# Mixers: four more output rows with seven block products instead of eight, and one ordered block for gate stage and output projection

## The chip, the cores and the metric

The kernel runs on 1 core of a Trainium2 chip. The metric is device time in microseconds (us) of one execution. The median of 3 runs of the kernel before is 2486.89 us (2486.2 to 2486.92).

The engines are named as the profile names them: PE (matmul; PEld is its weight load), DVE (elementwise on two operands), ACT (elementwise on one operand, with functions such as the sigmoid), POOL and SP (here nearly all of their work is the issue of transfers). Each works through its own queue in order and waits on semaphores for the others.

## What is computed

Two layers, each with a feed-forward half step, a mixer and a second feed-forward half step, on 640 tokens (512 of a prompt and 128 of running streams), width 1024. The change is in the mixer. Cut to what matters:

```python
z = h @ w_in                                   # conv B | conv C | conv V | q | k | v | gates
cb, cc, cv, q, k, v, g = split(z)
g_conv, g_attn = split(sigmoid(g + b_gate))    # 1024 columns each
y_conv = cb * causal_depthwise_conv3(cc * cv)  # 512 columns
y_attn = chunk_band_attention(q, k, v)         # 512 columns
m = g_conv * (y_conv @ w_conv_out) + g_attn * (y_attn @ w_attn_out)
x = x + m @ w_o
```

All of it is float32.

## The kernel before

**Layout.** Activations lie transposed: 128 features on the partitions, 640 tokens along the row. `x[m]` is the m-th of 8 such tiles (KT = 8), `y_conv` and `y_attn` have 4 (CT = 4). Weights come as a stream of 128 x 1024 "slabs", eight 128 x 128 blocks each, one transfer of 512 KB on SP's queue per slab.

**Three products for one.** Every float32 operand is split in two parts, `hi` (a rounded copy, made by ACT, "CAST whi") and `lo` (what is left, made by DVE, "wlo<-raw,whi"). A product is the sum hi·hi + hi·lo + lo·hi. A matmul instruction takes 128 x 128 weights and 320 tokens (HT, half of the row), so one weight block on all tokens is 6 instructions.

**Eight or seven block products.** A plain product (`product`, line 434) sums its weight blocks over all k. The other form treats a product as 2 x 2 blocks (even and odd feature tiles, first and second half of the tokens) and uses seven block products instead of eight, after Strassen and Winograd. It needs mixtures of the operand's quarters (names N6, T7, T4, T5) and of the weights. The weight mixtures are made by DVE on the two raw slabs of a group ("raw<-raw", "s<-raw,raw") and by POOL, which loads one slab onto another with an adding transfer ("one<-in_wst"). Such a group has 2 raw slabs and gives 4 prepared ones, where two plain slabs give 2.

**The gate stage** (`outputs`, one per layer, after the attention) is what changes. It works through, in this order:
- gate pairs: `gate_pair(m)` makes gates m and m+1 of the 16 from h. Seven block products of 12 instructions each on PE, into banks named qa, qb and qc. Gates 0 and 1 are made earlier.
- `out(m)`: one row tile of `y_conv @ w_conv_out` (m below 8) or `y_attn @ w_attn_out` (8 to 15), 24 instructions in bank py, then a multiplication by the gate and, for the attention, an addition into `mm[m - 8]`, both on DVE.
- `rows("co", (4, 5, 6, 7))`: the convolution's rows 4 to 7 at once, by seven block products: 84 instructions, banks rb, ra and rc.

The order before is: pair 2, out 0 to 3, pairs 4 and 6, `rows("co")`, then four times a pair and two outs (pair 8, out 8, out 9, and so on to out 15). `give` then splits the sums `mm` into hi and lo, as inputs of w_o. Last, the output projection: eight products `po` of 48 instructions each, each followed by an addition to x on DVE and by `ex.final(m)`, which prepares the next feed-forward's operands.

**What sets the order.** PE, DVE and ACT have their order written out by hand here (`manual_schedule`): their instructions stand in the queue as the code issues them. Callbacks put work between block products: `at[0..2]` in a gate pair, `due()` and `lates` for what is put off to the next unit. `prep` issues the next slab's casts on ACT, `flush` the pending lo parts on DVE, `ahead` and `source` the weight mixtures. The pool `tp` (tag t) has 4 temporaries for gates, `acc` has 2 double banks (py, po, ra, rb), `att` 4 banks.

**Names.** In listings raco and rbco are the banks of `rows("co")`, capsm, c and rs are staging tiles, ya and yc are `y_attn` and `y_conv` (yc tiles are used again as `mm[4..7]`), m_0hi is the hi part of m's tile 0, `thi` and `hhim` are operands of the gate pairs.

Of the kernel before, what the change touches and what calls it, by code (L numbers as in the profile page):

```python
# [11 lines left out]
F32R = mybir.dt.float32r  # L12
# [4 lines left out]
P = 128  # L17
# [178 lines left out]
def trunk(ctx: ExitStack, tc: tile.TileContext, xin, wst, small, pbias, samplebias, kcache, vcache, gfin,  # L196
# [1136 lines left out]
    def mixer(l, after):  # L1333
        with tc.tile_pool(name=f"yp{l}", bufs=1, reuse_waits="tile") as yp, \
# [83 lines left out]
            layout(f"g{l}", 1)  # L1418
            with tc.tile_pool(name=f"gp{l}", bufs=1, reuse_waits="tile") as gp, \
                 tc.manual_schedule(engines=ORDERED):  # L1420
# [3 lines left out]
        with tc.manual_schedule(engines=ORDERED):  # L1424
            hold[0] = True
            for m in range(KT):
                po = acc(f"po{l}_{m}")
                product(po, mo)
                ex.weights(m)
                DVE.tensor_tensor(out=halves(x[m]), in0=two(po), in1=halves(x[m]), op=ALU.add)  # L1430
                if m < KT - 1:
                    flush()
                ex.final(m)
        return ex
# [50 lines left out]
    def outputs(l, gp, X, st, cs, ycp, yas, sigmoid, gates):  # L1485
# [20 lines left out]
        def gate_pair(m, at):  # L1506
            n = f"{l}_{m}"
            pa, pb, pc = (att(f"q{i}{n}")[:, :HT] for i in "abc")
            u, g = gates[m], gates[m + 1] = tmp(f"g{n}"), tmp(f"g{n}_1")
            s0 = quiet()  # L1510
            block(pa, s0, 0, X11, every, True, True)
            ACT.copy(c1, pa)
            due()
            prep(used[0] + 1)
            flush()
# [51 lines left out]

        yc, ya, mo = [], [], []
        more = []
        yas_ = [yas[:, c, :] for c in range(CT)]  # L1570

# [3 lines left out]

        def give(ms):
            for m in ms:
                mo.append(parts(hp, "h", f"m{l}_{m}", mm[m]))

        def low(lo, z, hi):  # L1580
            DVE.tensor_tensor(out=lo, in0=z, in1=hi.bitcast(F32), op=ALU.subtract)

        def mixed(i, y, z):

            z = z.rearrange("p c (a b) -> p (c a) b", a=2)
            e1, e2, o1, o2 = (z[:, i] for i in range(4))
            add(e1, e1, e2, ALU.subtract)
            add(e2, o2, e2, ALU.subtract)
            for out, a in ((o2, e1), (o1, o2)):
                DVE.scalar_tensor_tensor(out=out, in0=a, scalar=-1.0, in1=out, op0=ALU.mult, op1=ALU.subtract)  # L1590
            yield
            hi, lo = (gp.tile([P, 3, HT], F32R, tag=f"x{i}{p}", name=f"x{p}{l}_{len(more)}") for p in ("hi", "lo"))
            ACT.copy(hi, z[:, 1:])
            more.append((hi, lo))
            yield
            low(lo, z[:, 1:], hi)
            yield
            hi, lo = (u[:, t2] for u in y[2 * i])
            ACT.copy(hi, e1)
            yield  # L1600
            low(lo, e1, hi)
            yield

        def take_even(c, src):
            y = tuple(gp.tile([P, T], F32R, tag=f"y{c}{i}", name=f"ya{l}_{c}{i}") for i in ("hi", "lo"))
            split(*(z[:, t1] for z in y), src[:, t1])
            ya.append(y)

        EXTRA = XT7, XT4, XN6

        def kind(y, i, k):
            if k in EXTRA:
                return tuple(z[:, EXTRA.index(k)] for z in more[i - 2])
            hi, lo = y[2 * i + (k in (X21, X22))]
            return tuple(z[:, t2 if k in (X22, XT5) else t1] for z in (hi, lo))

        def rows(name, ms, y, then=None):

# [7 lines left out]
            def mul(ps, s, half, k, start):  # L1626
                for u in range(2):
                    for i in range(2):
                        kp = half * NP + 2 * u + i
                        wh, wl = (z[:, kp * P : (kp + 1) * P] for z in s)  # L1630
                        xh, xl = kind(y, i, k)
                        for j, (w, x_) in enumerate(((wh, xh), (wh, xl), (wl, xh))):
                            PE.matmul(ps[u], w, x_, start=start and i == 0 and j == 0,
                                      stop=i == 1 and j == 2, skip_group_check=True)
# [18 lines left out]
            prep(used[0] + 1)  # L1653
            flush()
            mul(b, w, 1, X21, True)
            add(s1, two(B), s1)
# [3 lines left out]
            ACT.copy(s2, two(A))  # L1660
            gated(0, [s1[:, u] for u in range(2)], t1)
            mul(c, w, 1, XT5, True)
            for u in range(2):
# [5 lines left out]
            ahead()  # L1669
            gated(1, [s5[:, u] for u in range(2)], t2, -1.0)  # L1670
            mul(c, w, 1, X22, False)
# [3 lines left out]
            gated(0, [s2[:, u] for u in range(2)], t2)  # L1675
            if then:
                then()
            if name == "co":
                moved(0)
            mul(a, w, 0, XT4, False)  # L1680
            flush()
            gated(1, a, t1, -1.0)
            if name == "co":
                lates.append(lambda: moved(1))

        def total(m0, m1):
            for m in range(m0, m1):
                add(mm[m], mm[m], gates[KT + m])

        none = lambda: None  # L1690

        def also(*fs):
            return lambda: [f() for f in fs]

        def going(z):
            return lambda: next(z)

        gate_pair(2, [none, none, lambda: take(yc, "yc", range(CT), ycs)])
        z = [mixed(i, yc, ycp[i]) for i in range(2)]
        out(0, yc, None, going(z[0]))  # L1700
        out(1, yc, None, also(going(z[0]), going(z[1])))
        out(2, yc, None, also(going(z[0]), going(z[1])))
        out(3, yc, None, going(z[1]))
        both = also(going(z[0]), going(z[1]))
        gate_pair(4, [both, both, none])
# [665 lines left out]
```

## Time and profile before

| | us |
|---|---|
| median of 3 runs | 2486.89 |
| the profiled execution | 2487.08 |
| its span, first to last instruction | 2485.3 |
| PE busy | 2471.0 (99%) |
| DVE busy | 2158.3 (87%) |
| ACT busy | 1373.0 (55%) |
| POOL busy | 317.4 (13%) |

The profiled execution took 1.78 us more than its span and 0.19 us more than the median. Its mean granted PE clock is 0.999 of full speed. The gate stage and w_o of layer 0 lie at about 634 to 833 us of the span, those of layer 1 at about 1866 to 2064 us.

A matmul's row shows a start and a duration; matmuls overlap, so what one costs on a full PE is the distance from its start to the next start, not its duration. The same holds, to a smaller degree, for DVE and ACT. In a timeline, "[0.96 <-PE raco L1633]" after a row says how long the engine was idle before it, and what ended the wait.

### The profile page before, as it was taken

Reading aid. Unit: us, or ns where it says so; the run is one execution under the profiler, and the core shown is the slowest. Engines: PE = TensorE matmul, PEld = TensorE weight load, DVE = VectorE, ACT = ScalarE, POOL = GpSimd, SP = SyncE. Lnnn points to the kernel's source line nnn. Section 1 sums busy time; section 2 is a strip of 40 time slices with the busy share of each in tenths; the row PEclk is TensorE's granted clock in tenths of the full one; section 3 lists DMA queues with packets and bytes.
Section 4 is the critical chain, followed back from the end, with each engine's and each line's share of the span. In section 5 each row is a group of like instructions: output and inputs, shape, how many; then the busy total and the mean of one; then the engine's idle time right before and its main releaser. Section 6 shows DMA issues by size and latency. Waiting matters only on the chain.

```text
span 2485.3 us, 43991 instructions
## 1 busy us (share of the span) xinstructions
PE 2471.0 (99%) x17288; PEld 2418.2 (97%) x17288; DVE 2158.3 (87%) x3587; ACT 1373.0 (55%) x2196; POOL 317.4 (13%) x479
## 2 busy tenths in 40 slices
PE   9999999999999999999999999999999999999999
PEld 8999999889999999999999999998999999999998
DVE  7999998888886899998799999988878769999997
ACT  6555556665554555555665555556645455555555
POOL 0111112211000001111001111121110000111111
PEclk9999999999999999999999999999999999999999
DMA  4443445335343334444334443453453333443444
GB/s 155 126 118 102 123 119 121 113 109 177 104 118 108 94 101 106 112 117 120 108 94 109 110 118 102 116 128 107 132 173 92 115 111 89 107 116 106 113 117 117
DMA packets 113072, 287.11 MB, mean 116 GB/s; under 512 B 12928, under 2 KB 52480, under 8 KB 112864
## 3 DMA queue, kind: packets, MB, share of 16 engines
q1 hardware_dynamic: 69552, 220.10, 28.0%
q0 software_dynamic: 42880, 63.94, 13.7%
q8 instruction: 135, 2.21, 0.4%
q14 instruction: 73, 0.60, 0.1%
q10 hardware_dynamic: 432, 0.25, 0.0%
HBM read 238.43 MB, written 7.94 MB: 99 GB/s over the span
## 4 chain that ended last, share of the span: by engine, by line
PE 92%; DVE 4%; ACT 2%; DMA 1%; issue 1%; SPq 0%; DVEq 0%; ACTq 0%; POOLq 0%
PE pab L458 12%; PE paa L458 11%; PE pcb L458 6%; PE daa L1143 6%; PE pca L458 5%; PE dab L1143 5%; PE po L434 5%; PE qa L458 4%; PE py L434 3%; PE pbb L458 3%; PE dca L1143 3%; PE pba L458 3%; PE dcb L1143 2%; PE ma_qk L458 2%; PE ma_cv L458 2%; PE pv L1770 2%
## 5 line engine op out<-in xcount | busy, mean ns | idle before, releaser
L363 ACT CAST whi<-raw 128x512 fp32r<-128x512 f32 (+1 forms) x573 | 500.4, 878 | 371.3 <-PE pbb L458 46.0
L368 DVE TENSOR_TENSOR wlo<-raw,whi 128x512 fp32r<-128x512 f32 (+1 forms) x573 | 574.4, 1005 | 135.9 <-ACT whi L363 132.1
L363 ACT CAST whi<-s 128x1024 fp32r<-128x1024 f32 (+1 forms) x160 | 151.6, 947 | 313.3 <-issue 111.4
L458 PE MATMUL pab<-xhib,whi 128*128 128x320 f32 x704 | 217.5, 309 | 0.0
L458 PE MATMUL pab<-xlob,whi 128*128 128x320 f32 x704 | 217.0, 308 | 0.0
L458 PE MATMUL pab<-xhib,wlo 128*128 128x320 f32 x704 | 217.0, 308 | 0.0
L458 PE MATMUL paa<-xhia,whi 128*128 128x320 f32 x640 | 197.7, 309 | 0.2 <-DVE ga L295 0.2
L458 PE MATMUL paa<-xhia,wlo 128*128 128x320 f32 x640 | 197.5, 309 | 0.0
L458 PE MATMUL paa<-xloa,whi 128*128 128x320 f32 x640 | 197.4, 308 | 0.0
L368 DVE TENSOR_TENSOR wlo<-s,whi 128x1024 fp32r<-128x1024 f32 (+1 forms) x160 | 174.8, 1092 | 4.6 <-ACT whi L363 4.6
L1165 POOL DMA_DIRECT2D x<-c_a x80 | 70.0, 1022 | 573.8 <-ACT ahia L1047 205.5
L1165 POOL DMA_DIRECT2D x<-c_b x72 | 62.8, 1002 | 583.6 <-ACT ahib L1047 205.8
L458 PEld LDWEIGHTS pab<-xhib,whi 128*128 128x128 f32 x704 | 132.1, 188 | 0.9 <-issue 0.9
L458 PEld LDWEIGHTS pab<-xlob,whi 128*128 128x128 f32 x704 | 132.2, 188 | 0.0
L458 PEld LDWEIGHTS pab<-xhib,wlo 128*128 128x128 f32 x704 | 132.1, 188 | 0.0
L458 PEld LDWEIGHTS paa<-xhia,whi 128*128 128x128 f32 x640 | 120.1, 188 | 1.1 <-DVE ga L295 0.5
L458 PEld LDWEIGHTS paa<-xloa,whi 128*128 128x128 f32 x640 | 120.1, 188 | 0.2 <-DVE xloa L702 0.2
L458 PEld LDWEIGHTS paa<-xhia,wlo 128*128 128x128 f32 x640 | 120.1, 188 | 0.2
L295 DVE TENSOR_TENSOR raw<-s,raw 128x512 f32<-128x512 f32 x160 | 109.1, 682 | 0.0
L458 PE MATMUL pcb<-xhib,wlo 128*128 128x320 f32 x352 | 108.7, 309 | 0.0
L458 PE MATMUL pcb<-xlob,whi 128*128 128x320 f32 x352 | 108.5, 308 | 0.0
L458 PE MATMUL pcb<-xhib,whi 128*128 128x320 f32 x352 | 108.5, 308 | 0.0
(840 smaller groups left out, 8150.4 us busy)
## 6 DMA issues: line engine op xcount, KB each, us to landing
raw<-in_wst SPq DMA_DIRECT2D x375, 512.0 KB, 3.6
x<-c_a POOLq DMA_DIRECT2D x80, 160.0 KB, 4.6
x<-c_b POOLq DMA_DIRECT2D x72, 160.0 KB, 3.6
lent<-in_wst POOLq DMA_DIRECT2D x36, 256.0 KB, 3.9
kc<-in_kcache SPq DMA_DIRECT2D x32, 256.0 KB, 5.2
vc<-in_vcache SPq DMA_DIRECT2D x16, 512.0 KB, 4.8
one<-in_wst POOLq DMA_DIRECT2D x28, 256.0 KB, 4.1
x<-u_a POOLq DMA_DIRECT2D x40, 160.0 KB, 4.1
```

What stands on the lines that cost most here:

```text
L295: DVE.tensor_tensor(out=out, in0=a, in1=b, op=op)
L363: ACT.copy(hi[:, d], src[:, c])
L368: DVE.tensor_tensor(out=lo, in0=src, in1=hi.bitcast(F32), op=ALU.subtract)
L434: PE.matmul(ps[:, a, :HT], w, x[a] if isinstance(x, tuple) else x[:, a * HT : (a + 1) * HT], start=first and j == 0 and not seeded, stop=l ...
L458: PE.matmul(ps, a, b, start=start and kp == 0 and j == 0, stop=stop and kp == NP - 1 and j == 2, skip_group_check=True)
L1143: PE.matmul(ps[u], w, y, start=start and i == 0 and j == 0, stop=i == 1 and j == 2, skip_group_check=True)
L1165: POOL.dma_start(x[ms[2 * u + r]][:, cols], z[:, u], accum_op=ALU.add)
L1770: PE.matmul(pv[t], xx[:, t * P : (t + 1) * P], w[:, kk * AW : (kk + 1) * AW], start=c == 0 and kk == 0 and j == 0, stop=c == KT // 2 - 1 a ...
```

## The change

**Attention's rows 4 to 7 by seven.** `out(12)` to `out(15)` go. Pairs 12 and 14 follow each other, and `rows("ao", (4, 5, 6, 7))` stands after them. The mixtures of `y_attn` that it needs are made from its raw tiles in place (`mix`, four DVE instructions), and split into hi and lo (`high` on ACT, `rest` on DVE), all as callbacks of out 8 and of pairs 10, 12 and 14.

**Mixtures in tiles of their own.** Those of the convolution were one tile of three mixtures for each of two feature pairs; now each mixture has a tile that holds both pairs. For the convolution each is cast and split by itself (320 columns, six instructions on each engine, before two of 960).

**Sums and splits.** The sums of rows 4 to 7 are added after `rows("ao")` (`total`), those of m's tiles 0 to 3 are split earlier, in pair 14 and in `rows("ao")` (`given`).

**Copies.** `rows("co")` copies its four results from gate tiles to yc tiles (`moved`, on ACT). The first two copies used to stand before `qa_8`'s first copy; now they stand behind it, and the other two come in pair 8's second callback.

**w_o.** Gate stage and w_o are one ordered block. The first two products take their slabs together and run in two halves each: po_0 and po_1 with m's tiles 0, 2, 1, 3, then both with 4 to 7.

The number of raw slabs is the same; each layer has two more prepared slabs. Outside the gate stage and w_o the queues are the same, instruction by instruction.

```diff
-    for i in range(4):
+    for i in range(2):
         out += [gates[4 + i], ("ao", 2 * i), ("ao", 2 * i + 1)]
+    out += gates[6:] + [("rows", ("ao", (4, 5, 6, 7)))]
     return out + [("o", m) for m in range(KT)]
...
+        first = [acc(f"po{l}_{m}") for m in range(2)]
+        ws = [[tiles.take() for _ in mo] for _ in first]
+        for ks in ((0, 2, 1, 3), range(KT // 2, KT)):
+            for p, w in zip(first, ws):
+                for k in ks:
+                    multiply(p, w[k], mo[k], k == 0, k == KT - 1)
+        for m in range(KT):
+            po = first[m] if m < 2 else acc(f"po{l}_{m}")
+            if m > 1:
                 product(po, mo)
...
+        def room(name):
+            for k in EXTRA:
+                x[name, k] = tuple(gp.tile([P, 2, HT], F32R, tag=f"x{EXTRA.index(k)}{i}",
+                                           name=f"x{i}{name}{l}_{EXTRA.index(k)}") for i in ("hi", "lo"))
...
-            ACT.copy(hi, z[:, 1:])
-            more.append((hi, lo))
+            for k in EXTRA:
+                ACT.copy(x["co", k][0][:, i], z[:, 1 + EXTRA.index(k)])
...
+        za = yas.rearrange("p (i c) (a b) -> p i (c a) b", i=2, a=2)
+
+        def mix(n):
+
+            e1, e2, o1, o2 = (za[:, :, k] for k in range(4))
+            if n == 0:
+                add(e1, e1, e2, ALU.subtract)
+            elif n == 1:
+                add(e2, o2, e2, ALU.subtract)
+            else:
+                minus(*((o2, e1) if n == 2 else (o1, o2)))
+
+        def place(k):
+            if k == XT5:
+                return [(*(u[:, t2] for u in ya[2 * i]), za[:, i, 0]) for i in range(2)]
+            return [(*x["ao", k], za[:, :, 1 + EXTRA.index(k)])]
+
+        def high(*ks):
+            for k in ks:
+                for hi, _, z in place(k):
+                    ACT.copy(hi, z)
+
+        def rest(*ks):
+            for k in ks:
+                for hi, lo, z in place(k):
+                    low(lo, z, hi)
...
-            if name == "co":
-                moved(0)
...
             if name == "co":
-                lates.append(lambda: moved(1))
+                lates.append(lambda: moved(0))
+                moves.append(lambda: moved(1))
...
-        rows("co", (4, 5, 6, 7), yc)
-        for m in range(KT, 2 * KT, 2):
-            last = m == 2 * KT - 2
-            gate_pair(m, [none, none, (lambda: take(ya, "ya", range(CT), yas_)) if m == KT else
-                          (lambda: give(range(1))) if last else none])
-            out(m, ya, (lambda: give(range(1, 4))) if last else None)
-            out(m + 1, ya, (lambda: give(range(4, 6))) if last else None)
-        give(range(6, KT))
+        rows("co", (4, 5, 6, 7), None)
+        gate_pair(8, [none, moves[0], lambda: take(ya, "ya", range(CT), srcs)])
+        room("ao")
+        out(8, ya, None, lambda: mix(0))
+        out(9, ya)
+        gate_pair(10, [lambda: mix(1), lambda: (mix(2), high(XT7)), lambda: (mix(3), rest(XT7))])
+        out(10, ya)
+        out(11, ya)
+        gate_pair(12, [none, lambda: high(XN6, XT4), lambda: (rest(XN6, XT4), high(XT5))])
+        pre = lambda: rest(XT5)
+        gate_pair(14, [pre, lambda: (begun(*range(4)), given(0, 2)), none])
+        rows("ao", (4, 5, 6, 7), None, lambda: given(1, 3), None, True)
+        begun(*range(4, KT))
+        total(4, 5)
+        given(4)
+        total(6, 7)
+        given(5, 6, 7)
         return mo
```

**Place 1: ACT where pair 8 begins, right after `rows("co")`, layer 0.** Before: the first two yc copies stand ahead of the copy of qa_8, which empties the bank that PE's third block product of the pair adds to.

```order
L363 CAST whi_7964<-raw_7940 128x512
L1647 COPY yc_0_4819<-g_4_7588 128x640
L1647 COPY yc_0_4819<-g_4_1_7589 128x640
L1512 COPY capsm_4817<-qa_8_7988 128x320
L1647 COPY yc_1_4820<-g_6_7721 128x640
L1647 COPY yc_1_4820<-g_6_1_7722 128x640
L363 CAST whi_8009<-one_7810 128x512
L363 CAST whi_8009<-raw_7921 128x512
```

After:

```order
L364 CAST whi_7974<-raw_7950 128x512
L1520 COPY capsm_4817<-qa_8_7996 128x320
L1689 COPY yc_0_4819<-g_4_7611 128x640
L1689 COPY yc_0_4819<-g_4_1_7612 128x640
L364 CAST whi_8017<-one_7820 128x512
L364 CAST whi_8017<-raw_7931 128x512
L364 CAST whi_8036<-raw_7950 128x512
L1531 COPY capsm_4817<-qa_8_7996 128x320
L1533 COPY c_4829<-qc_8_7998 128x320
L1689 COPY yc_1_4820<-g_6_7746 128x640
L1689 COPY yc_1_4820<-g_6_1_7747 128x640
L364 CAST whi_8070<-raw_8068 128x1024
```

The copy of qa_8 now stands first, and the third and fourth yc copy have moved behind pair 8's later bank copies, ahead of the slab cast and the ya casts.

**Place 2: DVE from pair 12 to pair 14, layer 0.** In the rows, a wlo with an s operand (s_111, s_110) is the weight part that PE's third block product of pair 14 needs. Before, two outs lie between the pairs (py_12, py_13):

```order
L368 TENSOR_TENSOR wlo_8459<-raw_8456,whi_8458 128x1024
L295 TENSOR_TENSOR g_12_8391<-qc_12_8390,capsm_4817 128x320
L1536 TENSOR_TENSOR g_12_8391<-g_12_8391,rrm_4818 128x640
L1542 TENSOR_TENSOR g_12_1_8392<-qa_12_8388,rrm_4818 128x320
L368 TENSOR_TENSOR wlo_8492<-raw_8476,whi_8491 128x1024
L295 TENSOR_TENSOR raw_8512<-raw_8512 128x512
L295 TENSOR_TENSOR s_111_8514<-raw_8512,raw_8476 128x512
L1562 TENSOR_TENSOR g_12_8391<-py_12_8511,g_12_8391 128x640
L295 TENSOR_TENSOR yc_0_4819<-yc_0_4819,g_12_8391 128x640
L368 TENSOR_TENSOR wlo_8518<-s_111_8514,whi_8517 128x512
L368 TENSOR_TENSOR wlo_8518<-raw_8512,whi_8517 128x512
```

After:

```order
L369 TENSOR_TENSOR wlo_8483<-raw_8480,whi_8482 128x1024
L296 TENSOR_TENSOR raw_8500<-raw_8500 128x512
L296 TENSOR_TENSOR s_110_8505<-raw_8500,raw_8480 128x512
L1592 TENSOR_TENSOR xloao_2_8142<-ya_4760,xhiao_2_8141 128x640
L1592 TENSOR_TENSOR xloao_1_8140<-ya_4760,xhiao_1_8139 128x640
L296 TENSOR_TENSOR g_12_8426<-qc_12_8412,capsm_4817 128x320
L1545 TENSOR_TENSOR g_12_8426<-g_12_8426,rrm_4818 128x640
L1551 TENSOR_TENSOR g_12_1_8427<-qa_12_8410,rrm_4818 128x320
L369 TENSOR_TENSOR wlo_8526<-s_110_8505,whi_8525 128x512
L369 TENSOR_TENSOR wlo_8526<-raw_8500,whi_8525 128x512
```

The outs' multiplications and additions are gone from between the pairs, the weight mixtures (raw<-raw, s<-raw,raw) have moved up, and two splits of y_attn's mixtures (xloao) stand in the same run, ahead of the s part.

**Place 3: PE where w_o begins, layer 0.** Before, the last out of the gate stage runs into po_0, whose products take m's tiles in the order 0, 1, 2 and so on:

```order
L434 MATMUL py_15_8748<-ya_3lo,whi_8646 128x320 x2
L434 MATMUL py_15_8748<-ya_3hi,wlo_8647 128x320 x2
L434 MATMUL po_0_8804<-m_0hi,whi_8683 128x320 x2
L434 MATMUL po_0_8804<-m_0lo,whi_8683 128x320 x2
L434 MATMUL po_0_8804<-m_0hi,wlo_8684 128x320 x2
L434 MATMUL po_0_8804<-m_1hi,whi_8683 128x320 x2
L434 MATMUL po_0_8804<-m_1lo,whi_8683 128x320 x2
L434 MATMUL po_0_8804<-m_1hi,wlo_8684 128x320 x2
L434 MATMUL po_0_8804<-m_2hi,whi_8683 128x320 x2
L434 MATMUL po_0_8804<-m_2lo,whi_8683 128x320 x2
```

After:

```order
L1675 MATMUL raao_4_8688<-xloao_1_8140,whi_8726 128x320
L1675 MATMUL raao_4_8688<-xhiao_1_8139,wlo_8727 128x320
L435 MATMUL po_0_8850<-m_0hi,whi_8765 128x320 x2
L435 MATMUL po_0_8850<-m_0lo,whi_8765 128x320 x2
L435 MATMUL po_0_8850<-m_0hi,wlo_8766 128x320 x2
L435 MATMUL po_0_8850<-m_2hi,whi_8765 128x320 x2
L435 MATMUL po_0_8850<-m_2lo,whi_8765 128x320 x2
L435 MATMUL po_0_8850<-m_2hi,wlo_8766 128x320 x2
L435 MATMUL po_0_8850<-m_1hi,whi_8765 128x320 x2
L435 MATMUL po_0_8850<-m_1lo,whi_8765 128x320 x2
L435 MATMUL po_0_8850<-m_1hi,wlo_8766 128x320 x2
L435 MATMUL po_0_8850<-m_3hi,whi_8765 128x320 x2
```

The instructions in front are now those of `rows("ao")` (bank raao), and po_0 takes tiles 0, 2, 1 and then 3; po_1's first half comes before po_0's second.

More of the change, by code (lines that the diff above doesn't have):

```diff
@@ L1423, in mixer @@
         ex = after()
[L1424 to L1427, printed above, removed]
-                product(po, mo)
[L1429 to L1433, printed above, removed]
+        hold[0] = True
+        first = [acc(f"po{l}_{m}") for m in range(2)]
[7 more added lines that the diff above has]
+            if m > 1:
+                product(po, mo)
+            ex.weights(m)
+            DVE.tensor_tensor(out=halves(x[m]), in0=two(po), in1=halves(x[m]), op=ALU.add)
+            if m < KT - 1:
+                flush()
+            ex.final(m)
+        order.close()
         return ex
@@ L1566, in out @@
                 post()
-        yc, ya, mo = [], [], []
-        more = []
-        yas_ = [yas[:, c, :] for c in range(CT)]
+        yc, ya = [], []
+        mo = [None] * KT
+        srcs = [yas[:, c, :] for c in range(CT)]
+        x, moves = {}, []
         def take(y, name, cs, srcs):
@@ L1602, in mixed, with kind, rows @@
             yield
[L1604 to L1607, printed above, removed]
+        za = yas.rearrange("p (i c) (a b) -> p i (c a) b", i=2, a=2)
[19 more added lines that the diff above has]
+                    low(lo, z, hi)
         EXTRA = XT7, XT4, XN6
-        def kind(y, i, k):
+        def kind(name, i, k):
             if k in EXTRA:
-                return tuple(z[:, EXTRA.index(k)] for z in more[i - 2])
-            hi, lo = y[2 * i + (k in (X21, X22))]
+                return tuple(z[:, i] for z in x[name, k])
+            hi, lo = (yc if name == "co" else ya)[2 * i + (k in (X21, X22))]
             return tuple(z[:, t2 if k in (X22, XT5) else t1] for z in (hi, lo))
-        def rows(name, ms, y, then=None):
+        def rows(name, ms, first, mid=None, late=None, end=False, defer=False):
             n = f"{name}{l}_{ms[0]}"
@@ L1654, in rows @@
             flush()
+            if first:
+                first()
             mul(b, w, 1, X21, True)
@@ L1669, in rows @@
             ahead()
-            gated(1, [s5[:, u] for u in range(2)], t2, -1.0)
+            if defer:
+                moves.append(lambda: gated(1, [s5[:, u] for u in range(2)], t2, -1.0))
+            else:
+                gated(1, [s5[:, u] for u in range(2)], t2, -1.0)
+            if late:
+                late()
             mul(c, w, 1, X22, False)
@@ L1690, in outputs, with total, begun, given @@
+            if end:
+                flush()
+        def total(*ms):
+            for m in ms:
+                add(mm[m], mm[m], gates[KT + m])
+        def begun(*ms):
+            for m in ms:
+                mo[m] = tuple(hp.tile([P, T], F32R, tag=f"h{i}", name=f"m{l}_{m}{i}") for i in ("hi", "lo"))
+        def given(*ms):
+            for m in ms:
+                split(*mo[m], mm[m])
         none = lambda: None
[L1692 to L1696, printed above, removed]
+        def going(*zs):
+            return lambda: [next(z) for z in zs]
```

54 lines of the change are left out of this document (29 added, 25 removed).

## The prediction

> **What bounds the kernel now.** First the page's busy times, then PE's waits.
>
> ```profile
> span 2485.3 us, 43991 instructions
> PE 2471.0 (99%) x17288; PEld 2418.2 (97%) x17288; DVE 2158.3 (87%) x3587; ACT 1373.0 (55%) x2196; POOL 317.4 (13%) x479
> PE poa L434 <- ACT whi L758: 5.6, 1, 5.6
> ```
>
> PE is busy for all but 14 us of the span, and its longest wait, 5.6 us, is the program's start. So time goes down by PE instructions that fall away and by small stalls between its rows, and up where PE is made to wait. What a PE instruction costs, the stretches of time tell: pair 6, `rows("co")`, and out 8 with out 9.
>
> ```profile
> 674.10:686.42 12.32, 12.32 (x87) 12.32 (x86) 9.15 (x16) 6.37 (x11) 1.43 (x2) 1.00 0.33 112
> 686.42:698.72 12.30, 12.30 (x85) 12.30 (x85) 10.29 (x18) 7.23 (x12) 1.43 (x2) 1.00 0.49 130
> 711.46:718.50 7.04, 7.04 (x50) 7.04 (x49) 6.94 (x11) 2.67 (x5) 0.00 (x0) 1.00 0.43 108
> ```
>
> The columns are the stretch's length, then busy time of PE, PEld, DVE, ACT and POOL, and the granted clock. The code issues 84, 84 and 48 instructions there (the counts include some that reach in from the sides). 12.32 / 84 and 7.04 / 48 are both 146.7 ns. That is the price, not the 309 ns of a row. `rows("co")`, the form that the change adds again, runs here at full PE speed with DVE 84% busy.
>
> **Term 1, the instructions.** Out 12 to 15 are 4 x 24 = 96 instructions, 14.08 us by the third row. `rows("ao")` is 84, 12.32 us. That is 1.76 us less per layer, 3.52 us in all.
>
> By the Trainium skill ("TensorE: Matmul & The Clock Gate", section "Back-to-back issue gap") the spacing is N / 2.4 + 2.5 ns, 135.8 ns for 320 columns; term 1 would then be 3.26 us, an estimate. The trace's 146.7 ns is 8% above that, and decides.
>
> **Term 2, stalls that go.** PE's timeline at three places, start and duration first:
>
> ```profile
> 702.09 0.31 PE L458 MATMUL qb<-hhim,wlo 128*128 128x320 f32 x1
> 702.52 0.41 PE L458 MATMUL qa<-thi,whi 128*128 128x320 f32 x1
> 702.77 0.31 PE L458 MATMUL qa<-tlo,whi 128*128 128x320 f32 x1
> ...
> 776.23 0.46 PE L434 MATMUL py<-ya_3hi,wlo 128*128 128x320 f32 x2
> 776.75 0.53 PE L434 MATMUL po<-m_0hi,whi 128*128 128x320 f32 x2
> 777.12 0.45 PE L434 MATMUL po<-m_0lo,whi 128*128 128x320 f32 x2
> ...
> 782.10 0.46 PE L434 MATMUL po<-m_6hi,whi 128*128 128x320 f32 x2
> 782.46 0.56 PE L434 MATMUL po<-m_6lo,whi 128*128 128x320 f32 x2
> 782.86 0.45 PE L434 MATMUL po<-m_6hi,wlo 128*128 128x320 f32 x2
> ```
>
> A single instruction should be 0.147 us from the next, a double one 0.293. Pair 8's third block product starts 0.28 late and its second instruction another 0.10: 0.38. Po_0 loses 0.23 + 0.08 = 0.31, and at m_6lo 0.07 + 0.11 = 0.18. What stood before them on ACT (first two rows) and DVE (third):
>
> ```profile
> 700.79 1.35 ACT L1647 COPY yc<-g 128x640 f32<-128x640 f32 x2 [0.78 <-DVE g L1640]
> 702.05 0.41 ACT L1512 COPY capsm<-qa 128x320 f32<-128x320 f32 x1
> 775.79 0.82 DVE L1562 TENSOR_TENSOR g<-py,g 128x640 f32<-128x640 f32 x1
> ```
>
> The copy of qa ends at 702.46, just before PE goes on: it waited behind the two yc copies, which now stand behind it (place 1). That stall goes. Po_0 needed the bank of out 14, read by DVE until 776.61, behind the splits of m's tiles 1 to 3; now its bank is rb, read in the middle of `rows("ao")`. That stall goes too. The third goes if m's last splits come in time, which the next part works out. Both layers run the same code; I count the first two twice and the third once: 0.76 + 0.62 + 0.18 = 1.56 us.
>
> **Term 3, new waits.** Pairs 12 and 14 and `rows("ao")` now follow each other as pairs 4 and 6 and `rows("co")` do, so DVE's rows of pair 6 show the pace, and PE's row when the part is needed:
>
> ```profile
> 683.16 0.49 DVE L295 TENSOR_TENSOR g<-qa,c 128x320 f32<-128x320 f32 x1 [2.39 <-PE qa L458]
> 683.68 0.49 DVE L1529 TENSOR_TENSOR g<-g,rrm 128x320 f32<-128x320 f32 x1
> 684.09 1.22 DVE L368 TENSOR_TENSOR wlo<-raw,whi 128x1024 fp32r<-128x1024 f32 x1
> 685.23 0.69 DVE L295 TENSOR_TENSOR raw<-raw 128x512 f32<-128x512 f32 x1
> 685.95 0.69 DVE L295 TENSOR_TENSOR s<-raw,raw 128x512 f32<-128x512 f32 x1
> 686.56 0.48 DVE L295 TENSOR_TENSOR g<-qc,capsm 128x320 f32<-128x320 f32 x1
> 687.07 0.82 DVE L1536 TENSOR_TENSOR g<-g,rrm 128x640 f32<-128x640 f32 x1
> 687.82 0.48 DVE L1542 TENSOR_TENSOR g<-qa,rrm 128x320 f32<-128x320 f32 x1
> 688.22 0.68 DVE L368 TENSOR_TENSOR wlo<-s,whi 128x512 fp32r<-128x512 f32 x1
> ...
> 690.22 0.31 PE L1633 MATMUL raco<-xhi,wlo 128*128 128x320 f32 x1
> ...
> 646.55 0.82 DVE L235 TENSOR_TENSOR yc_0lo<-yc,yc_0hi 128x640 fp32r<-128x640 f32 x1
> 647.28 0.82 DVE L235 TENSOR_TENSOR yc_1lo<-yc,yc_1hi 128x640 fp32r<-128x640 f32 x1
> ```
>
> From the release at 683.16 DVE runs without a gap; the s part is ready at 688.90 and needed at 690.22, 1.32 us of slack. In pair 12 two splits of 640 columns stand in this run (place 2), 0.735 us each from start to start: 1.47 us. The s part of pair 14 comes 0.15 us late; with 0.15 for the semaphore and the restart (by the 0.10 that PE lost after the 0.28 above) I take 0.3 per layer, 0.6 in all. Its ends are 0 (the run is 0.15 shorter somewhere) and 1.47 (no slack).
>
> Everything else I cost at nothing, and name the cover:
> - Mixtures 0 to 2 of y_attn, 3 x 0.74 = 2.2 us, stand before pair 10's release at 727.56, where DVE idles 2.76 (row below); 0.5 stays. Mixture 3 and T7's split (1.47) lie ahead of a slab split that PE needs only after out 10 and out 11, 7.04 us later.
> - T5's splits (2 x 0.40) and those of m's tiles 0 and 2 (1.47) stand before pair 14's release: 2.27 of the 2.39 at 683.16, which the late run before has already eaten into. Adding up the same rows, DVE reads the bank about 0.7 after its release; the last block product needs the read (0.49 long) done after 12 x 0.147 = 1.76, so some 0.2 to 0.5 is left: the thinnest place.
> - The convolution's six splits for two are 6 x 0.40 against 2 x 1.07, 0.26 us more, before an idle of 1.27 at 670.86.
> - Pair 8's other two yc copies, 1.26 us by the 1.35 above less overlap, now stand before a slab cast at 706.66 and the ya casts. The cast then ends at 708.97; DVE wants it at 709.15. Below zero is excluded, since nothing on PE waited there.
> - The end: after the last block product DVE reads the banks (an estimated 1.0 of backlog, by adding up the rows of `rows("co")` and the two splits more, then 2 x 0.40), splits a slab (1.14), adds (0.74) and, after a cast of 0.72, splits tile 4: 4.7 us. PE gets there after half of po_0 and of po_1, 7.04 us. Tile 5's split follows at 7.6, needed at 7.04 + 0.88 + 0.29 = 8.2; 6 and 7 later. Po_1's bank is free at 2.1, needed at 3.5.
> - SP has as many slabs as before. POOL has one more adding pair of transfers per layer, at the distance that pairs 4, 6 and `rows("co")` have.
>
> ```profile
> 662.61 1.15 DVE L1581 TENSOR_TENSOR xlo<-yc,xhi 128x960 fp32r<-128x960 f32 x1
> 663.68 0.82 DVE L1560 TENSOR_TENSOR mm<-py,g 128x640 f32<-128x640 f32 x1
> ...
> 668.70 0.48 DVE L1581 TENSOR_TENSOR yc_0lo<-yc,yc_0hi 128x320 fp32r<-128x320 f32 x1
> 669.10 0.48 DVE L1581 TENSOR_TENSOR yc_2lo<-yc,yc_2hi 128x320 fp32r<-128x320 f32 x1
> 670.86 0.49 DVE L295 TENSOR_TENSOR g<-qa,c 128x320 f32<-128x320 f32 x1 [1.27 <-PE qa L458]
> ...
> 706.66 1.05 ACT L363 CAST whi<-raw 128x1024 fp32r<-128x1024 f32 x1
> 707.61 0.72 ACT L234 CAST ya_0hi<-ya 128x640 fp32r<-128x640 f32 x1
> ...
> 709.15 1.22 DVE L368 TENSOR_TENSOR wlo<-raw,whi 128x1024 fp32r<-128x1024 f32 x1
> ...
> 727.56 0.49 DVE L295 TENSOR_TENSOR g<-qa,c 128x320 f32<-128x320 f32 x1 [2.76 <-PE qa L458]
> ```
>
> **Sum.** -3.52 - 1.56 + 0.60 = -4.48 us. The profiled execution of 2487.08 us becomes 2482.6; it lies 0.19 above the median of 2486.89, so I forecast 2482.4 us, 0.18% less. That is just inside the 0.2% (5.0 us) which is about what a measurement of this kernel can tell from no change.
>
> **Rivals.**
> *The thin places eat the gain.* Four points per layer have under 1 us of slack: pair 14's s part, its last block product, the same in `rows("ao")`, tile 5's split. At 0.5 us more each that is 2 x 2.0 = 4.0 us: 2486.4. For it: a late DVE row delays a sigmoid on ACT and so the next slab's cast. Against: `rows("co")` has the same chain without a loss.
>
> *DVE is slow on mixtures in place (slower).* They read and write 2 x 320 columns out of ya's rows. If such a row took e us more, pair 10 would be 3e - 0.5 late and pair 14's s part 0.3 + 2e: 10e - 0.4 over both layers, hence 2481.4 + 10e. It is slower than before from e = 0.55, by over 0.2% from 1.05; at 1.2 it gives 2493.4. Against it: an output in two pieces, the first and third of three, costs no more than one piece (818 ns against 820):
>
> ```profile
> L1034 DVE TENSOR_TENSOR deb<-ub,gb x18: 814/818/825, 851.9 to 2392.3; 128x640 f32<-128x640 f32 x18
> ```
>
> *DVE instructions don't overlap.* If each started only when the one before had ended, pair 6's run and the two splits would take 6.04 (the nine durations) + 1.64 = 7.68 us from the release, against 7.06 to the need: 0.62 late, 0.32 more than I took per layer: 2483.0. The rows speak against it: 0.735 apart at 0.82 long. The Trainium skill says it ("VectorE: DVE Perf Modes", section "The DRAIN you can't avoid": the next op does not start until the pipe is empty); by that rule this rival holds, and the trace disagrees.
>
> *An instruction is worth its 309 ns.* Then term 1 is 7.4 us: 2478.5. The 146.7 ns above speak against it. That the change does not drop the instructions can be left out: place 3 shows `rows("ao")` in the outs' place.
>
> **Chances and range.** Forecast 0.64 (its own range 2481.4 to 2484); thin places 0.18; no overlap 0.04; 309 ns 0.03; slow mixtures 0.11, with whatever else makes DVE late there. The range 2480.8 to 2487.0 leaves out the 309 ns, nearly all of the slow mixtures and a little of the forecast's tails, under 0.2. Faster by over 0.2% means below 2481.9: the 309 ns and, of the forecast, the part without new waits, 0.22: 0.25. Slower by over 0.2%: 0.08 of the 0.11. Within: 0.67.
>
> **What would show it.** 24 fewer PE instructions, at 147 ns. In pair 8 no step before the third block product; in po_0 none at its first instructions and at tile 6. A step of about 0.3 us at the third block product of pair 14, released by DVE. DVE idle before pair 10's release down to some 0.5 us. I am wrong if PE shows steps of a microsecond between pair 10 and po_1, if mixtures in place take over 0.82 us, or if time moves outside the gate stage and w_o.

## The result, and the profile after

| | us, median | lowest to highest | runs |
|---|---|---|---|
| before | 2486.43 | 2485.99 to 2487.37 | 20 |
| changed | 2482.2 | 2481.64 to 2482.89 | 20 |

The changed kernel takes 0.9983 of the time, 95% interval 0.9976 to 0.999: 4.23 us less. The forecast was 2482.4 us, and within 0.2% as the likeliest class. The profiled execution of the changed kernel took 2481.95 us.

The head of the changed kernel's page:

```profile
span 2480.2 us, 44054 instructions
PE 2467.0 (99%) x17264; PEld 2414.6 (97%) x17264; DVE 2182.4 (88%) x3643; ACT 1385.6 (56%) x2230; POOL 319.5 (13%) x483
```

PE has 24 instructions fewer (17288 to 17264) and 4.0 us less busy time. DVE got 56 instructions and 24.1 us more, ACT 34 and 12.6 us more, and but for the step at pair 14 below PE waits no longer for either: their extra work found room beside PE. The longest wait is still the start of the program.

Where the time went, PE's timeline tells: the gate stage and w_o run from the first instruction of pair 2 to the first `pab` of the next feed-forward. First before, then the changed kernel, layer 0 and layer 1:

```profile
635.42 0.31 PE L458 MATMUL qa<-hhim,whi 128*128 128x320 f32 x1
...
833.30 0.31 PE L458 MATMUL pab<-xhib,whi 128*128 128x320 f32 x1
...
1866.62 0.41 PE L458 MATMUL qa<-hhim,whi 128*128 128x320 f32 x1 [0.66 <-ACT ya L1988]
...
2064.65 0.31 PE L458 MATMUL pab<-xhib,whi 128*128 128x320 f32 x1
```

```profile
635.54 0.31 PE L459 MATMUL qa<-hhim,whi 128*128 128x320 f32 x1
...
831.18 0.31 PE L459 MATMUL pab<-xhib,whi 128*128 128x320 f32 x1
...
1863.76 0.31 PE L459 MATMUL qa<-hhim,whi 128*128 128x320 f32 x1
...
2059.41 0.31 PE L459 MATMUL pab<-xhib,whi 128*128 128x320 f32 x1
```

Layer 0 goes from 197.88 to 195.64 us, layer 1 from 198.03 to 195.65: 2.24 and 2.38 less, 4.62 together. The spans differ by 5.1. Of the rest, 0.74 lies between the stages (1033.32 to 1032.58), and the stretches ahead of the first stage and behind the second are 0.12 and 0.14 longer. The 0.74 is in the main the wait on `ya` in before's third row (0.66 us of idle time; the row starts 0.82 later than on a full PE), which the changed kernel's third row doesn't have. The instruction behind it starts another 0.10 late, inside before's stage. The wait comes in some executions and not in others: of the other profiled executions below, e1's has it (0.62 us), and e6's and e7's, which are the kernel before with one edit each, do not. So it isn't the change's. Without the 0.82 and the 0.10 the two profiles differ by about what the medians do.

The places that the prediction named, on PE in layer 0 of the changed kernel: pair 8's third block product, that of pair 14, po_0's start, and po_0's second half from tile 5 to tile 6.

```profile
702.22 0.31 PE L459 MATMUL qb<-hhim,wlo 128*128 128x320 f32 x1
702.36 0.31 PE L459 MATMUL qa<-thi,whi 128*128 128x320 f32 x1
702.51 0.31 PE L459 MATMUL qa<-tlo,whi 128*128 128x320 f32 x1
...
753.49 0.31 PE L459 MATMUL qa<-tlo,whi 128*128 128x320 f32 x1
753.85 0.41 PE L459 MATMUL qa<-thi,wlo 128*128 128x320 f32 x1
754.10 0.31 PE L459 MATMUL qa<-thi,whi 128*128 128x320 f32 x1
...
774.82 0.45 PE L435 MATMUL po<-m_0hi,whi 128*128 128x320 f32 x2
775.11 0.46 PE L435 MATMUL po<-m_0lo,whi 128*128 128x320 f32 x2
...
783.36 0.46 PE L435 MATMUL po<-m_5hi,wlo 128*128 128x320 f32 x2
783.66 0.46 PE L435 MATMUL po<-m_6hi,whi 128*128 128x320 f32 x2
783.95 0.46 PE L435 MATMUL po<-m_6lo,whi 128*128 128x320 f32 x2
```

At pair 8 and at po_0 the rows are 0.15 (single) and 0.29 (double) apart: the steps of 0.38 and 0.31 us are gone, and so is the one at tile 6 (783.66 to 783.95). At pair 14 a new one stands: 753.85 is 0.21 late and 754.10 another 0.10. Layer 1 has the same (0.21 and 0.10). Two small ones are new in both layers: m's tile 5 (783.36 comes 0.04 late, its like in layer 1 0.07), and 0.03 at the last block product of `rows("ao")`.

The rows of DVE that the prediction reckoned with: a mixture in place, the next one's row and the release of pair 10, the run of pair 14's weights in pair 12, and the split of m's tile 5.

```profile
719.84 0.82 DVE L296 TENSOR_TENSOR ya<-ya 128x640 f32<-128x640 f32 x1
720.57 0.81 DVE L1571 TENSOR_TENSOR g<-py,g 128x640 f32<-128x640 f32 x1
...
727.25 0.49 DVE L296 TENSOR_TENSOR g<-qa,c 128x320 f32<-128x320 f32 x1 [0.54 <-PE qa L459]
...
749.99 1.55 DVE L1592 TENSOR_TENSOR xloao<-ya,xhiao 128x640 fp32r<-128x640 f32 x2
751.46 0.48 DVE L296 TENSOR_TENSOR g<-qc,capsm 128x320 f32<-128x320 f32 x1
751.97 0.82 DVE L1545 TENSOR_TENSOR g<-g,rrm 128x640 f32<-128x640 f32 x1
752.72 0.48 DVE L1551 TENSOR_TENSOR g<-qa,rrm 128x320 f32<-128x320 f32 x1
753.12 0.68 DVE L369 TENSOR_TENSOR wlo<-s,whi 128x512 fp32r<-128x512 f32 x1
...
782.09 0.82 DVE L236 TENSOR_TENSOR m_5lo<-yc,m_5hi 128x640 fp32r<-128x640 f32 x1
```

A mixture in place costs 0.82 us like any row of 640, and the next starts 0.73 later. DVE's idle time before pair 10's release is 0.54 (2.76 before). The part of the weights that pair 14 needs is ready at 753.80, and PE goes on with it at 753.85: the two splits (1.47 us from their start to the next) stand in the run.

### The profile page after: what moved, and what is told of

Its sections match the earlier page's. It is cut to its first block, busy times and chain, and to the rows that moved or that the text cites. A ratio compares the mean times of both kernels' runs of the same rounds, so it can differ in the third digit from the quotient of the medians.

```text
span 2480.2 us, 44054 instructions
## 1 busy us (share of the span) xinstructions
PE 2467.0 (99%) x17264; PEld 2414.6 (97%) x17264; DVE 2182.4 (88%) x3643; ACT 1385.6 (56%) x2230; POOL 319.5 (13%) x483
## 4 chain that ended last, share of the span: by engine, by line
PE 93%; DVE 3%; ACT 2%; issue 1%; DMA 1%; SPq 0%; DVEq 0%; ACTq 0%; POOLq 0%
PE pab L459 12%; PE paa L459 11%; PE pcb L459 6%; PE daa L1144 6%; PE pca L459 5%; PE dab L1144 5%; PE po L435 5%; PE qa L459 4%; PE pbb L459 3%; PE dca L1144 3%; PE pba L459 3%; PE dcb L1144 2%; PE ma_cv L459 2%; PE ma_qk L459 2%; PE py L435 2%; PE pv L1835 2%
```

## The experiments

The theory: PE is full, so the change is worth its 24 instructions at 146.7 ns, plus the stalls that go, less the step at pair 14. The rivals: an instruction is worth another price; the stalls are due to something else than the rows named. Medians are compared with the changed kernel's 2482.2 us or with before's of the same runs (2486.44 to 2486.53).

### e1: the splits one callback earlier

```diff
-        gate_pair(12, [none, lambda: high(XN6, XT4), lambda: (rest(XN6, XT4), high(XT5))])
+        gate_pair(12, [lambda: high(XN6, XT4), lambda: rest(XN6, XT4), lambda: high(XT5)])
```

> The changed kernel with one edit: the two splits of y_attn's mixtures in pair 12 (1.47 us of DVE per layer) stand ahead of pair 12's release, where DVE idles 3.83 us, and no longer behind it. My theory (the s part of pair 14 comes late by exactly these two splits): PE's step of 0.31 us at the third block product of pair 14 is gone in both layers, DVE's idle time before pair 12's release falls from 3.83 to about 2.3, and the time falls by 0.6 us against the changed kernel. Rival (the s part is late for another reason, ACT's cast or the raw slab): the step stays at 0.31.

Measured: 2481.52 us (2481.16 to 2482.47, 11 runs), 0.68 less; 0.998 of before, interval 0.9971 to 0.9989. PE's timeline of e1, at pair 14's third block product:

```profile
753.28 0.31 PE L459 MATMUL qa<-tlo,whi 128*128 128x320 f32 x1
753.42 0.31 PE L459 MATMUL qa<-thi,wlo 128*128 128x320 f32 x1
```

The step is gone in both layers, and the stages are 0.31 and 0.20 us shorter (195.33 and 195.45; the second has the 0.10 behind the `ya` wait in it, which this execution had and the changed kernel's had not). DVE's idle time right before pair 12's release falls from 3.83 to 1.67 us. So the two splits in the run are its whole cause. This version beats both kernels; it has the lowest median of those that leave nothing out.

### e3: the same splits twice

```diff
-lambda: (rest(XN6, XT4), high(XT5))
+lambda: (rest(XN6, XT4, XN6, XT4), high(XT5))
```

> The changed kernel with the two splits of pair 12 issued twice (the second time they write the same values): 1.47 us more of DVE per layer in the place that I called the critical run. My theory: the slack is used up there, so PE's step at pair 14's third block product grows from 0.31 to about 1.8 us and the time by 2 x 1.47 = 2.9 us. Rival (DVE catches up, or the step has another cause): the step stays near 0.3 and the time within 0.5 us of the changed kernel. A second rival (late DVE rows delay ACT's sigmoids and casts, and the lateness grows): more than 4 us.

Measured: 2484.79 us (2484.36 to 2485.86), 2.59 more. The stages are 197.12 and 197.13, 1.48 more each, which is one more pair of splits at 0.735 us each. PE's timeline of e3:

```profile
756.32 0.42 PE L459 MATMUL qa<-thi,wlo 128*128 128x320 f32 x1 [1.52 <-DVE wlo L369]
```

There is no slack left at this place: what DVE gets ahead of that split, PE waits out in full. By the stages that is 2.96 us, the 2.9 expected; the medians differ by 0.4 less, and why is open.

### e2 and e6: the yc copies put back, and moved alone

e2 is the changed kernel with the copies where they were; e6 is the kernel before with only the copies moved.

```diff
 # e2
+            if name == "co":
+                moved(0)
             mul(a, w, 0, XT4, False)
...
-                lates.append(lambda: moved(0))
-                moves.append(lambda: moved(1))
+                lates.append(lambda: moved(1))
...
-        gate_pair(8, [none, moves[0], lambda: take(ya, "ya", range(CT), srcs)])
+        gate_pair(8, [none, none, lambda: take(ya, "ya", range(CT), srcs)])
```

> The changed kernel with the yc copies of rows(co) put back where they were: two ahead of pair 8's first bank copy, two behind it. My theory: PE's steps of 0.28 and 0.10 us at the third block product of pair 8 come back in both layers, 0.76 us in all against the changed kernel. Rival (the step had another cause, such as weights that came late): no step, no difference.

> The kernel before with the yc copies alone moved as in the change. My theory: PE's steps at pair 8's third block product go (0.38 us per layer), nothing else changes: 0.76 us less than before. Rival (the two later copies delay the ya casts and out 8): no gain, with a new step at out 8.

Measured: e2 2483.08 us (2482.59 to 2483.63), 0.88 more than the changed kernel. e6 2485.87 (2485.46 to 2486.87), 0.66 less than before's 2486.53. PE's timeline of e2 shows the step again (the row before starts at 702.21):

```profile
702.64 0.41 PE L459 MATMUL qa<-thi,whi 128*128 128x320 f32 x1
702.90 0.31 PE L459 MATMUL qa<-tlo,whi 128*128 128x320 f32 x1
```

That is 0.28 + 0.11, and e6 has no step there. With the copies in their old place the fifth block product of pair 8 has a small step of its own (0.05 in e2's two layers, 0.05 and 0.04 in the kernel before), which e6 and the changed kernel don't have; so e2's stages are 0.46 and 0.45 longer. The copies make the stall at pair 8, whichever of the two kernels they stand in, and nothing took its place.

### e4: 48 instructions fewer

The changed kernel with the products 2 to 7 of w_o short of one instruction in three for two of their eight weight blocks. What is left out is lo(w_o)·hi(m) for the features of m's tiles 0 and 1 there, a part of the precision. No operand is left unmade.

```diff
-                product(po, mo)
+                for k in range(KT):
+                    multiply(po, tiles.take(), mo[k], k == 0, k == KT - 1, cut=k < 2)
```

> The changed kernel without the lo*hi instructions of k = 0 and 1 in w_o's products 2 to 7, so that part of the precision of m @ w_o is left out: 4 instructions in each of 6 products and 2 layers, 48 in all. My theory (an instruction on a full PE is worth its distance to the next, 146.7 ns): 7.0 us less than the changed kernel. Rival (it is worth the 309 ns of its row): 14.8 us less. By the page's 135.8 ns: 6.5 us less.

Measured: 2475.56 us (2475.48 to 2476.06, 5 runs), 6.64 less, 138 ns for each of 48. The stages tell it apart: 192.12 and 192.13 us, 3.52 less in each layer, which is 24 x 146.7 ns to the digit. The rest is what comes next. PE's timeline of e4, then of the changed kernel, in the feed-forward behind w_o:

```profile
834.65 0.31 PE L459 MATMUL pcb<-xlob,whi 128*128 128x320 f32 x1
835.24 0.41 PE L459 MATMUL pcb<-xhib,wlo 128*128 128x320 f32 x1 [0.28 <-DVE wlo L369]
```

```profile
838.36 0.31 PE L459 MATMUL pcb<-xlob,whi 128*128 128x320 f32 x1
838.56 0.41 PE L459 MATMUL pcb<-xhib,wlo 128*128 128x320 f32 x1
```

With w_o 3.52 us shorter, a weight split on DVE is late by 0.44 us instead of 0.05, in both layers: 0.78 us handed back, 6.26 left. The medians differ by 6.64; single executions differ by some tenths. Had I divided the median alone by the instructions, I would have come out at 138 ns, near the 135.8 ns by the Trainium skill's formula for an isolated matmul ("TensorE: Matmul & The Clock Gate", section "Back-to-back issue gap", an estimate); the stage length says that an instruction is worth 146.7 ns here.

### e7: w_o's first two products in halves, alone

The kernel before, with only the new w_o loop.

```diff
+            first = [acc(f"po{l}_{m}") for m in range(2)]
+            ws = [[tiles.take() for _ in mo] for _ in first]
+            for ks in ((0, 2, 1, 3), range(KT // 2, KT)):
+                for p, w in zip(first, ws):
+                    for k in ks:
+                        multiply(p, w[k], mo[k], k == 0, k == KT - 1)
```

> The kernel before with w_o's first two products in halves as in the change, and the gate stage as it was. My theory: the step at tile 6 goes (0.18 us in layer 0, 0.10 in layer 1), but po_1 now needs the bank of out 15 at 780.3 us, and DVE reads it until 780.8: a new step of about 0.6 us per layer; po_0's step of 0.31 stays, since its bank is out 14's. So 0.8 to 1.0 us longer than before. Rival (the halves are a gain by themselves): 0.3 us or more shorter than before.

Measured: 2487.59 us (2487.06 to 2489.41), 1.06 more than before. The step at tile 6 goes, but PE's timeline has a new one where po_1 starts (the row before, a double one, starts at 781.09):

```profile
781.90 0.56 PE L434 MATMUL po<-m_0hi,whi 128*128 128x320 f32 x2 [0.35 <-DVE g L1569]
782.30 0.45 PE L434 MATMUL po<-m_0lo,whi 128*128 128x320 f32 x2
```

It loses 0.52 + 0.11 us per layer and wins 0.18 in layer 0 and 0.16 in layer 1. Po_0's own step of 0.31 stays, as expected. Po_1 now starts half a product earlier than before, and its bank is that of out 15, which DVE reads late. In the changed kernel both banks come from `rows("ao")`, and neither product has a step where it starts.

### e5 and e9: w_o in the old order, in both layers and in layer 0

The changed kernel, with po_0 whole and then po_1.

```diff
-        first = [acc(f"po{l}_{m}") for m in range(2)]
...
+        for m in range(KT):
+            po = acc(f"po{l}_{m}")
+            product(po, mo)
```

> The changed kernel with w_o's first two products in the old order: po_0 over m's tiles 0 to 7, then po_1. By the changed kernel's trace DVE ends the splits of tiles 4, 5, 6 and 7 at 780.7, 782.9, 783.6 and 784.4 us, and po_0 starts at 774.8. My theory: po_0 then waits for tile 4 and for tile 5, 3.5 us in each layer, so the time is 7 us longer than the changed kernel's, more than the whole gain. Rival (the order of the first products matters little, since DVE is done in time): under 1 us.

> The changed kernel, with the first two products of w_o in layer 0 one after the other as wholes (waits of 1.4, 0.3 and 1.1 us there), and in halves in layer 1. With both layers plain the runs fell into two groups, 2490.9 to 2491.6 and 2493.2 to 2494.0 us, and the profiled one, of the lower group, shows the lower clock in one layer only. If each layer's waits cost 3.5 us and each dip another 2.1 us, and the dip comes in some executions and not in others, one plain layer gives two groups: 2485.7 us without the dip and 2487.8 us with it. If the excess over 3.5 us per layer were something else that the plain order brings every time (longer waits, a late transfer), there is one group, at about 2487.5 us, half of the 11.05 us over the changed kernel.

Measured: e5 2493.25 us (2490.88 to 2493.95), 11.05 more, against 7.0 expected. Its 11 runs lie in two groups, four from 2490.88 to 2491.58 and seven from 2493.2 to 2493.95. The stages of the profiled execution, one of the lower group (2491.58), are 199.16 and 201.22: 3.52 more in layer 0, as expected, and 5.57 in layer 1. PE's timeline of e5, layer 0 and then layer 1:

```profile
780.41 0.56 PE L435 MATMUL po<-m_4hi,whi 128*128 128x320 f32 x2 [1.43 <-ACT m_4hi L235]
781.27 0.56 PE L435 MATMUL po<-m_4lo,whi 128*128 128x320 f32 x2 [0.30 <-DVE m_4lo L236]
...
783.48 0.56 PE L435 MATMUL po<-m_5lo,whi 128*128 128x320 f32 x2 [1.06 <-DVE m_5lo L236]
...
2012.19 0.56 PE L435 MATMUL po<-m_4hi,whi 128*128 128x320 f32 x2 [1.41 <-ACT m_4hi L235]
2013.05 0.90 PE L435 MATMUL po<-m_4lo,whi 128*128 128x320 f32 x2 [0.30 <-DVE m_4lo L236]
...
2015.26 0.90 PE L435 MATMUL po<-m_5lo,whi 128*128 128x320 f32 x2 [0.24 <-DVE m_5lo L236]
...
2019.15 0.73 PE L435 MATMUL po<-m_7hi,wlo 128*128 128x320 f32 x2
2019.69 0.53 PE L435 MATMUL po<-m_0hi,whi 128*128 128x320 f32 x2
```

The first two waits are the same in both layers, and po_0 starts without a step in both. But from 2013.05 to 2019.69 a double row that does not wait takes 0.533 us instead of 0.293, and the third wait is 0.24 us in place of 1.06, since PE comes to it later. The stretches of time of e5 say why (the clock is the number behind POOL's):

```profile
781.00:787.00 6.00, 4.67 (x30) 4.41 (x31) 4.77 (x8) 2.52 (x5) 1.44 (x2) 1.00 0.76 227
...
2016.00:2019.70 3.70, 3.70 (x16) 3.70 (x16) 0.67 (x1) 0.18 (x1) 0.13 (x1) 0.50 0.41 115
2019.70:2025.00 5.30, 5.30 (x37) 5.30 (x37) 2.45 (x3) 3.14 (x4) 0.73 (x1) 0.99 0.59 144
```

PE was granted half its clock for 6.7 us. Layer 1 is 2.06 us longer for it than layer 0, the shorter third wait set off.

e9 measured 2487.04 us (2485.43 to 2488.81), 4.84 more. Three of its 11 runs are at 2485.4 to 2486.1, where the waits alone would put them; the others spread from 2486.5 to 2488.8, not in a clean group at 2487.8. The profiled execution (2487.05) has the lower clock in layer 0 now, from 783.06 to 786.4, 3.4 us. Its stage is 200.79, 3.52 for the waits and 1.63 for the clock; layer 1, in halves, has 195.64. The three slowest runs show a mean granted clock of 0.998, the other eight 0.999. So in the two profiled executions the extra comes with waits of the plain order, by the clock, for 3.4 or 6.7 us. That it comes in some executions and not in others is read from the times, and from e5, whose layer 0 has the waits without it; e9's three low runs have no trace. That e5's upper group had it in both layers fits the numbers, but that group has no trace.

### e8: the same splits three times

```diff
-lambda: (rest(XN6, XT4), high(XT5))
+lambda: (rest(*(XN6, XT4) * 3), high(XT5))
```

> The changed kernel, with the split of T4's last 640 columns done three times over instead of once (same result each time, two of them to no purpose). With it done twice, the step at the third block product of pair 14 grew from 0.31 us to 1.78 us in each layer and the kernel by 2.6 us. If a wait costs TensorE only its own length, thrice gives another 1.47 us per layer, a step of 3.25 us and 5.5 to 5.9 us over the changed kernel's 2482.2: 2487.7 to 2488.1 us. If a wait of about 3 us brings the lower clock that the plain w_o shows in layer 1 (granted clock 0.50 for 6.7 us, 2.06 us lost), each layer in which it comes adds up to 2.1 us: 2489.8 with one, 2491.9 to 2492.3 with both, and the trace has TensorE rows at a granted clock of 0.50 behind the step.

Measured: 2490.83 us (2490.36 to 2492.48), 8.63 more; none of the 11 runs is near the 2488 of the waits alone. PE's timeline of e8 in layer 0, and two of its stretches of time:

```profile
756.93 0.42 PE L459 MATMUL qa<-thi,wlo 128*128 128x320 f32 x1 [3.00 <-DVE wlo L369]
...
758.41 0.47 PE L459 MATMUL qa<-tlo,whi 128*128 128x320 f32 x1
758.67 0.47 PE L459 MATMUL qa<-thi,wlo 128*128 128x320 f32 x1
```

```profile
758.00:761.00 3.00, 3.00 (x13) 3.00 (x12) 2.93 (x7) 1.50 (x3) 0.00 (x0) 0.50 0.17 38
761.00:764.00 3.00, 3.00 (x22) 3.00 (x21) 1.17 (x3) 2.00 (x4) 0.00 (x0) 0.94 0.83 292
```

The step is the 3.25 us expected (3.16 late and, for the instruction behind it, 0.10), and the lower clock comes behind it in both layers, for some 3.4 us each. The stages are 200.14 and 200.26, 4.50 and 4.61 more: 2.95 from the wait and about 1.6 from the clock. I had taken 2.1 from e5's 6.7 us; the sum with 1.6 is 2491.3, with the profiled execution at 2491.28 and the median 0.45 lower.

## Why the prediction was right, step by step

- **Term 1** (-3.52 us, 24 instructions at 146.7 ns). Right. 24 instructions fell away, and e4 measures the price at 146.7 ns where nothing interferes. The rival with 309 ns, which would make e4 14.8 us faster, falls. The 135.8 ns that the prediction sets beside it is the wrong figure for this stream: the section of the Trainium skill that it names ("TensorE: Matmul & The Clock Gate", "Back-to-back issue gap") gives that formula for an isolated matmul, and says that in a stream of weight loads and matmuls, as here, both set the spacing.
- **Term 2** (-1.56 us). The mechanism at pair 8 is right: e2 brings its step back and e6 takes it away, each alone. Po_0's step goes with the gate stage and not with the order of w_o: it stays in e7 and is gone in e5. That it was the bank of out 14 is read from the rows and not varied. The term was undersized. I counted tile 6's step in layer 0 only, but layer 1 of the kernel before has 0.16 us there too:

```profile
2013.45 0.46 PE L434 MATMUL po<-m_6hi,whi 128*128 128x320 f32 x2
2013.80 0.56 PE L434 MATMUL po<-m_6lo,whi 128*128 128x320 f32 x2
2014.19 0.45 PE L434 MATMUL po<-m_6hi,wlo 128*128 128x320 f32 x2
```

I also overlooked the small step of pair 8's fifth block product (0.05 and 0.04). By its steps the term is 0.77 + 0.09 + 0.63 + 0.34 = 1.83 us. What takes tile 6's step away is w_o in halves: alone (e7) it brings a worse one at po_1, and without it (e5) the changed kernel loses 3.52 us per layer and more. So tile 6's 0.34 us is a gain only with the two parts together; the order of w_o by itself takes the step away and loses more than it wins.
- **Term 3** (+0.60 us). Right in place, cause and size: 0.31 us per layer, gone in e1, grown by a whole pair of splits in e3. Beside it two of the thin places lost a little: tile 5 0.04 and 0.07 us, `rows("ao")` 0.03 in each layer.
- **Costed at nothing.** Pair 10's mixtures left 0.54 us of idle (0.5 forecast). The last block product of pair 14 came without a step. The reckoning of the end was too short, and its cover hid it: the split of tile 4 ended 5.9 us after po_0's first row where 4.7 was forecast (its terms, with 0.74 for the split, add up to 5.1; needed at 7.04), that of tile 5 at 8.1 where 7.6 was forecast (782.09 + 0.82 against 774.82; needed at 8.2). That tile 5 cost next to nothing was luck in part.
- **The sum.** By the steps: -3.52 - 1.83 + 0.79, and -0.10 for the slow instruction behind the `ya` wait, which lies in before's stage: -4.66. The stages measure -4.62, the forecast was -4.48, and the medians differ by 4.23. That the forecast time came out only 0.2 us high is luck in part: it started from a median of three runs, 2486.89, which is 0.46 above that of 20, and took off 0.25 more than the medians show. Inside the sum, the stalls that went were 0.27 more than forecast, and the new ones 0.19 more.
- **The rivals.** Thin places that eat the gain (2486.4): 0.17 us beside the forecast step, in place of 4.0. Slow mixtures in place: 0.82 us a row, no excess. DVE without overlap (2483.0): in the run above, rows of 0.48 and 0.82 us are followed after 0.40 and 0.75. Their step at pair 14 would have been 0.62; it is 0.31. For this rival the prediction gave half of what the Trainium skill states ("VectorE: DVE Perf Modes", section "The DRAIN you can't avoid"): the section goes on that a next op that is not held starts earlier, and so leaves room for the overlap of these rows.

## What to carry to other kernels

On a full PE an instruction is worth the distance to the next start, and a saved one counts in full where the stage ends; compare lengths of stages, since a shortened stage can hand some of it back behind its end, where the next stage's preparation is late. A reordering that frees a resource earlier is tied to what held that resource: w_o in halves costs 1.06 us alone and is needed with the rest. Put preparation ahead of a deadline by the callback, not by the average load: with DVE 88% busy, moving two splits by a third of a pair was worth 0.68 us.

## What the runs showed of the hardware

- After waits on PE the granted clock can fall to 0.50, with starts about 0.267 us apart instead of 0.147 (e5: 0.533 for a double row), for about 3.4 us (e8, e9) or 6.7 us (e5). That cost 1.6 us (e8, e9) or, a shorter wait set off, 2.1 (e5). It came behind a single wait of 3.0 us in both layers of e8's profile, behind waits of 1.4 and 0.3 us in layer 1 of e5, and behind 1.4, 0.3 and 1.1 us in e9's layer 0; but not in e5's layer 0, with 1.4, 0.3 and 1.1 us too, nor in e3 with one of 1.5 us. So a long stall can cost one and a half times its length: in e8, 4.5 us for 2.95.
- By the Trainium skill ("TensorE: Matmul & The Clock Gate", section "What's actually happening") the clock is halved after at least one idle window of about 3.4 us and comes back after a busy one, with windows that run freely. The halving and the lengths of one and two windows agree with these traces, and windows that run freely would explain why the same waits bring it in one layer and not in another. That a window must be idle throughout does not agree: in e5 PE was idle for 1.41 and 0.30 us, with two instructions in between, when the clock fell, and in e8 for 3.0 us.
